# A one-layer transformer trunk on one core: norm steps handed out at other places, weight sums formed elsewhere, second attention's outputs written straight into their operand buffers

## The chip, the cores and the metric

The kernel runs on 1 core of a Trainium2 chip. The metric is the device time of one execution in microseconds (us). TensorE is PE in the profile, VectorE DVE, ScalarE ACT, GpSimd POOL, and SyncE SP; SP issues nearly all DMAs, POOL those that add to what lies at their destination.

## The reference, cut to what matters

One layer, 2048 frames, model width 1024, 16 heads of 64, feed-forward width 2816, all float32:

```python
def reference(x, g_pre_mix, g_post_mix, w_qkv, w_o, rel_bias, g_pre_ffn, g_post_ffn, w_gate, w_up, w_down):
    h = rms_norm(x, g_pre_mix[0])
    m = chunk_relpos_attention(h, w_qkv[0], w_o[0], rel_bias[0])
    x = x + rms_norm(m, g_post_mix[0])
    h = rms_norm(x, g_pre_ffn[0])
    return x + rms_norm(swiglu(h, w_gate[0], w_up[0], w_down[0]), g_post_ffn[0])
```

In the attention a chunk of 64 frames reads itself and the 8 chunks before it, with a learned bias per relative position and head: `softmax(q k / 8 + bias) v`. `swiglu` is `(silu(h w_gate) * (h w_up)) w_down`.

## The kernel before, in words

**Data.** Activations lie transposed (features on the 128 partitions) in four blocks of 512 frames, two blocks to a group `g`. A float32 product is made of three matmuls (`products`, L182): each operand is split into a rounded part `hi` and the rest `lo` (ScalarE writes `hi`, VectorE `lo`: `split`, L273, and for weights `split_part`, L129).

**Stages, in the order of TensorE.** First group: its queries, keys and values, with its attention beside them (`attend_first`, L1573, 56 to 500 us). Then output projection `o_half(0, 0)`; queries and keys of the second group (`qk_stage`, L927, about 522 to 755 us) and its values (`v_stage`, L986, to about 831 us). Second group's attention (`attend_second`, L1610, about 851 to 1256 us) with `o_half(0, 1)` beside it; `o_half(1, 0)` and `o_half(1, 1)` (to 1325 us). Then, for each group, gate and up (`gate_up`, L1059: 1325 to 1777 and 1980 to 2413 us) and down (`down`, L1152).

**Seven products for eight.** The big products (second group's queries, keys, values; gate and up; down) treat 2x2 blocks of weights A and of activations B by Strassen's scheme in Winograd's form: seven block products, named by their B side, B11, B21, T1, T2, B22, T3, T4. Four of them need sums of weight blocks: S1 = A21 + A22, S3 = A11 + A21, S2 = A11 + S1, S4 = A12 + S2. `weight_sums` (L852) makes these in DRAM: SP copies one block to the place of the sum, and POOL issues a DMA that adds the other block (`accum_op`) and has to wait for the copy. The generator gives 4 steps to each unit of weights, and whoever calls `next(sums)` issues one step, that is some copies and some additions. The units come in the order: 4 of queries and keys, 2 of values, 11 of gate and up, 11 of down. 40 steps are issued in the first attention, 8 in `qk_stage`, 14 in `v_stage`, two in three slots of the second attention (43), and the rest after it. An addition on POOL's queue is placed behind the last instruction of POOL so far, in the attentions a normalisation of probabilities (L489).

**Steps beside TensorE.** TensorE's order is written out by hand; the other engines' orders come from a scheduler which sees the program as it is written. Work that isn't matmul is handed out through the queue `later` (L190): `tick(w)` credits 1 for each product of 512 columns, and a step is written down when the credit reaches its cost. `drain()` (L202) writes down all that is left at once. `Late` (L1247) is the norm behind a projection: 8 steps `sums` (load a row of blocks, square, add up), `rstd` (two TensorE instructions at `pssq` and `prs` with a power on POOL between them, and `wait` units between the two), and 8 steps `write` (load output and residual, two vector operations, store, and with `keep` a square and an addition for the next norm). Small tiles come from rings: `io` has 3 buffers, `scratch` and `narrow` 9 in the feed-forward phase, the combined tiles of a stage lie in one `big` tile with a single buffer.

**The second attention.** 64 slots `t`, four query blocks `ib` for each of 8 pairs of heads and two blocks of frames. In a slot TensorE makes the scores (`st`, one buffer of three banks), VectorE adds the bias and takes the maximum (L481), ScalarE takes the exponential and its sum (L485), VectorE the reciprocal (L488), POOL multiplies (L489). Two slots later TensorE transposes the rows (`deep_transposed`, L540) and three slots later multiplies them with the values into the one bank `po` (`deep_output`, L563). `put` (L581) takes a finished `po`: it copies it to DRAM, to be loaded and split by `gather` (L592) when the projection is near; only the last pair goes straight into the operand buffers `ats`. `fill(t)` (L1546) interleaves `t` us of dense work. After each slot come 4 units of credit.

The kernel's code, as far as the change touches it:

## Time and profile before

| | |
|---|---|
| median of 3 runs | 2641.21 us (2634.43 to 2641.94) |
| profiled execution, its own time | 2643.79 us |
| its span | 2641.8 us |
| granted clock of TensorE, mean | 0.958 |
| busy share of the span: PE, DVE, ACT, POOL | 92%, 58%, 41%, 12% |
| moved by DMA | 564.51 MB, mean 214 GB/s |

How to read the rows that follow in the prediction. A row of a table by stretch gives the stretch in us, its length, and for each engine its busy time and number of instructions; then TensorE's granted clock (1.00 is full), the mean busy share of the core's 16 DMA engines, and GB/s. A row of waits reads: who waited at which line, for whom, us in total, times, longest. A row of a group gives line, engine, operation, out<-in, shapes, count, then busy us, the mean ns of one, and the engine's idle time before them with what ended it. A row of a timeline gives start, duration, what, and in brackets the idle time before. A matmul of 512 columns is listed with some 0.39 us, but the next one starts about 0.23 us after it, so matmuls are priced by stretches here.

### The profile page before, as it was taken

The numbers are of one execution on the slowest core, as the hardware profiler recorded it, in microseconds if no ns is written. First come the engines' busy times: TensorE is split into PE (matmuls) and PEld (weight loads), VectorE is DVE, ScalarE is ACT, GpSimd is POOL, SyncE is SP. The second block draws the span as 40 slices with busy tenths as digits, with TensorE's granted clock in tenths as the row PEclk, the third lists the DMA queues.
The fourth block names the chain that finished last, engine by engine and source line by source line (L and its number), as shares of the span: only waits on it lengthen the run. The fifth ranks groups of instructions, "written<-read, shape, count | busy, mean of one in ns | idle before, by whom it ended". The sixth has DMA issues, their size and how long they took to land.

```text
span 2641.8 us, 36015 instructions
## 1 busy us (share of the span) xinstructions
PE 2422.0 (92%) x12794; PEld 2011.7 (76%) x12794; DVE 1526.5 (58%) x2624; ACT 1091.7 (41%) x1913; POOL 321.0 (12%) x411
## 2 busy tenths in 40 slices
PE   9999998926998889479979999999999999999997
PEld 8887886715887778467768878888888888888886
DVE  6655546554544446465755675557765665555567
ACT  5444444332342446345343333336543333333444
POOL 0222222100000344233100000000000000000001
PEclk9999999967999989779989999999999999999999
DMA  7779889776899999895955675537757764456654
GB/s 219 198 209 252 209 232 254 210 232 187 264 302 263 255 229 232 231 253 130 285 183 186 223 247 179 161 119 247 251 196 234 244 207 156 151 159 219 199 186 153
DMA packets 247266, 564.51 MB, mean 214 GB/s; under 512 B 27920, under 2 KB 38176, under 8 KB 246832
## 3 DMA queue, kind: packets, MB, share of 16 engines
q1 hardware_dynamic: 230960, 515.03, 61.2%
q0 software_dynamic: 16128, 47.19, 11.0%
q8 instruction: 101, 1.65, 0.3%
q14 instruction: 77, 0.63, 0.1%
HBM read 432.30 MB, written 199.02 MB: 239 GB/s over the span
## 4 chain that ended last, share of the span: by engine, by line
PE 71%; DMA 14%; DVE 6%; issue 4%; ACT 2%; SPq 1%; POOL 1%; DVEq 0%; POOLq 0%; ACTq 0%
PE pd L185 6%; PE pd L186 6%; PE pd L184 6%; PE pb L184 5%; PE pb L185 5%; PE pb L186 5%; PE pa L184 3%; PE pa L186 3%; PE pa L185 3%; PE pc L184 3%; PE pc L186 3%; PE pc L185 3%; PE mm L184 3%; PE mm L185 3%; PE mm L186 3%
## 5 line engine op out<-in xcount | busy, mean ns | idle before, releaser
L485 ACT ACTIVATE sc<-sc,nmax 128x640 f32<-128x640 f32 (+4 forms) x256 | 193.0, 755 | 155.5 <-DVE nmax L481 146.3
L481 DVE CUSTOM_DVE_ANT_0 sc<-st,bias 128x640 f32<-128x640 f32 (+4 forms) x256 | 180.4, 738 | 129.4 <-PE st L473 115.1
L489 POOL TENSOR_SCALAR sc<-sc,rows 128x640 f32<-128x640 f32 (+4 forms) x256 | 200.2, 844 | 388.7 <-DVE rows L488 337.2
L184 PE MATMUL pb<-hb,whi_gate_up_at_T 128*128 128x512 f32 x528 | 207.1, 392 | 7.3 <-DVE terms L1104 7.3
L185 PE MATMUL pb<-hb,whi_gate_up_at_T 128*128 128x512 f32 x528 | 206.2, 390 | 0.0
L186 PE MATMUL pb<-hb,wlo_gate_up_at_T 128*128 128x512 f32 x528 | 206.0, 390 | 0.0
L184 PE MATMUL mm<-hb,whi 128*128 128x512 f32 x448 | 186.7, 417 | 0.0
L472 PE MATMUL st<-k,q 128*128 128x384 f32 (+1 forms) x448 | 140.3, 332 | 41.1 <-DVE nmax L481 29.2
L186 PE MATMUL mm<-hb,wlo 128*128 128x512 f32 x448 | 176.4, 394 | 1.6 <-DVE wlo L131 1.6
L185 PE MATMUL mm<-hb,whi 128*128 128x512 f32 x448 | 176.3, 394 | 0.0
L184 PE MATMUL pa<-hb,whi_gate_up_at_B 128*128 128x512 f32 x352 | 139.6, 397 | 12.4 <-ACT terms L1085 11.6
L258 POOL TENSOR_TENSOR rs<-ms,neg_half 128x4 f32<-128x4 f32 (+1 forms) x9 | 11.8, 1312 | 1128.4 <-DVE ms L256 1128.4
L186 PE MATMUL pa<-hb,wlo_gate_up_at_B 128*128 128x512 f32 x352 | 138.9, 395 | 3.9 <-DVE wlo_gate_up_at_B L131 3.9
L185 PE MATMUL pd<-a,whi_d_T 128*128 128x512 f32 (+1 forms) x368 | 139.9, 380 | 0.4 <-DVE a L275 0.4
L184 PE MATMUL pd<-a,whi_d_T 128*128 128x512 f32 (+1 forms) x368 | 140.0, 380 | 0.0
L186 PE MATMUL pd<-a,wlo_d_T 128*128 128x512 f32 (+1 forms) x368 | 139.7, 380 | 0.0
L185 PE MATMUL pa<-hb,whi_gate_up_at_B 128*128 128x512 f32 x352 | 138.7, 394 | 0.0
L473 PE MATMUL st<-k,q 128*128 128x384 f32 (+1 forms) x448 | 134.4, 319 | 0.0
L131 DVE TENSOR_TENSOR wlo_gate_up_at_T<-raw,whi_gate_up_at_T 128x1024 fp32r<-128x1024 f32 x88 | 107.5, 1221 | 41.2 <-ACT whi_gate_up_at_T L130 40.9
L130 ACT ACTIVATE whi_gate_up_at_T<-raw 128x1024 fp32r<-128x1024 f32 x88 | 93.1, 1058 | 91.3 <-PE pa L185 35.2
L1106 ACT ACTIVATE terms<-terms 128x512 f32<-128x512 f32 x66 | 41.7, 631 | 203.1 <-DVE terms L1104 203.1
L184 PEld LDWEIGHTS pb<-hb,whi_gate_up_at_T 128*128 128x128 f32 x528 | 99.5, 189 | 29.9 <-DVE terms L1104 9.4
(282 smaller groups left out, 6131.7 us busy)
## 6 DMA issues: line engine op xcount, KB each, us to landing
raw<-gu_S SPq DMA_DIRECT2D x88, 512.0 KB, 3.9
raw<-in_w_gu SPq DMA_DIRECT2D x66, 512.0 KB, 4.0
y<-y SPq DMA_DIRECT2D x96, 256.0 KB, 3.7
gu_S<-in_w_gu SPq DMA_DIRECT2D x44, 512.0 KB, 8.1
raw_d<-d_S SPq DMA_DIRECT2D x88, 256.0 KB, 3.4
raw_a<-aT SPq DMA_DIRECT2D x88, 256.0 KB, 3.5
aT<-T SPq DMA_DIRECT2D x66, 256.0 KB, 4.1
raw_a<-aB SPq DMA_DIRECT2D x66, 256.0 KB, 3.7
```

Source lines behind the costliest of these rows:

```text
L130: act.activation(hi, raw, AF.Copy)
L131: dve.tensor_tensor(lo, raw, hi.bitcast(F32), op=ALU.subtract)
L184: pe.matmul(pt, a_hi, b_hi, start=first, stop=False, skip_group_check=go_on)
L185: pe.matmul(pt, a_hi, b_lo, start=False, stop=False, skip_group_check=go_on)
L186: pe.matmul(pt, a_lo, b_hi, start=False, stop=last, skip_group_check=go_on)
L258: pool.tensor_tensor(r[0][:, :nb], m[:, :nb], neg_half.to_broadcast([P, nb]), op=ALU.pow)
L472: pe.matmul(st[:, a:b], q[:, 2 * h, cols], kk[:, h, key], start=True, stop=False)
L473: pe.matmul(st[:, a:b], q[:, 2 * h + 1, cols], kk[:, h, key], start=False, stop=True)
L481: dve.tensor_tensor_reduce(out=sc[:, :n], in0=st[:, c0 : c0 + n], in1=rev, scale=-1.0, scalar=3.0e38, op0=ALU.add, op1=ALU.min, accum_out= ...
L485: act.activation(sc[:, :n], sc[:, :n], AF.Exp, bias=nmax, scale=-1.0, accum_out=rows[:, 0:1])
L489: last_pool[0] = pool.tensor_scalar(sc[:, :n], sc[:, :n], rows[:, 1:2], 1.0, op0=ALU.mult, op1=ALU.mult)
L1106: act.activation(terms[0], terms[0], AF.Silu)
```

## The change

Five things, by the places where they stand.

1. **Norm of the first block's output.** In `dense`, the steps of `late` were put behind B22 in `later`, and `drain()` in the first unit of `qk_stage` wrote them down in one go. Now `qk_stage` gets `late` and puts its steps into `later` behind that `drain()`. The norm of the second block (`late1`) costs 4.0 and 8.0 per step, not 2.0 and 3.0; the norms in gate and up wait 24.0, not 6.0, between their two TensorE instructions.
2. **Sums of queries and keys.** No longer in `weight_sums` and DRAM: `qk_stream` loads the four blocks of a unit and VectorE adds them in place, four additions of 128x1024 a unit. `combined` takes two of its inputs from `narrow` instead of `io`.
3. **The other sums' places.** 40 steps in the first attention as before (now of values and gate and up), four products of a unit in `qk_stage` call for one instead of two (16 steps), `v_stage` once instead of twice for each product (7), the second attention not at all, the first group's `gate_up` at B11, T1, T2, T3 (what is left of 104 steps, down's units but for the start of the first three).
4. **Second attention's outputs.** The buffers `ats` of block (1, 0) exist from the start of the second attention, those of (1, 1) from the end of `o_half(0, 1)`. `put` splits each output straight into them from `po`, and what was spilled before that, for (1, 1), is gathered as before. The dense work runs at 1.2 us a slot instead of 0.8, 12 us of it ahead instead of 8.
5. **Reciprocals.** In the second attention one reciprocal for both heads of a slot, behind both exponentials; both normalisations stand behind it.

```diff
-sum_qk = {n: dram.tile([P, NPAIR // 2, 1024], F32, name=f"qk_{n}") for n in ("S1", "S2", "S3", "S4")}
...
 def scores(self, ib):
-                    sc[:, :n], sc[:, :n], AF.Exp, bias=nmax, scale=-1.0, accum_out=rows[:, 0:1]
+                    sc[:, :n], sc[:, :n], AF.Exp, bias=nmax, scale=-1.0, accum_out=rows[:, h : h + 1]
                 )
-                dve.reciprocal(rows[:, 1:2], rows[:, 0:1])
+                if g == 0:
+                    dve.reciprocal(rows[:, 2 + h : 3 + h], rows[:, h : h + 1])
+                elif h == 1:
+                    dve.reciprocal(rows[:, 2:4], rows[:, 0:2])
+            for h in range(2):
+                sc = self.sc[ib, h]
                 last_pool[0] = pool.tensor_scalar(
-                    sc[:, :n], sc[:, :n], rows[:, 1:2], 1.0, op0=ALU.mult, op1=ALU.mult
+                    sc[:, :n], sc[:, :n], rows[:, 2 + h : 3 + h], 1.0, op0=ALU.mult, op1=ALU.mult
                 )
...
 def put(self, po):
-            if p < NPAIR - 1 or (g, s) == (0, 1):
+            if (g, s) not in ats:
+                spilled[g, s].append(p)
                 ot = xp.tile([P, HALF], F32, tag="io", name="ot", bufs=3)
...
 def combined(self, w):
-                c[k] = [io("b11"), io("b12"), self.wait[:, k, :], self.wait[:, 4 + k, :]]
+                c[k] = [narrow("b11"), narrow("b12"), self.wait[:, k, :], self.wait[:, 4 + k, :]]
...
-    units = [qk_at(c) for c in range(NPAIR // 2)] + [v_at(u) for u in range(2)]
+    units = [v_at(u) for u in range(2)]
...
+    def qk_stream(c):
+        def add(out, a, b_):
+            dve.tensor_tensor(raw[out], raw[a], raw[b_], op=ALU.add)
...
+        makes = (
+            (("A11",), maker("B11", "A11")),
+            (("A12",), maker("B21", "A12")),
+            (("A21", "A22"), maker("T1", "A21", ("A11", "A11", "A21"), ("A21", "A21", "A22"))),
+            ((), maker("T2", "A21", ("A21", "A11", "A22"), ("A12", "A12", "A21"))),
+            ((), maker("B22", "A12")),
+            ((), maker("T3", "A11")),
+            ((), maker("T4", "A22")),
+        )
...
 def qk_stage(b, late):
-            if name in ("B22", "T4"):
+            if name in ("B11", "T1", "B22", "T4"):
                 next(sums, None)
...
             if c == 0:
                 drain()
+                later.extend(late.sums(8.0) + late.rstd(40.0) + late.write(10.0))
...
 def gate_up(g, b):
+            if g == 0 and name in ("B11", "T1", "T2", "T3"):
+                next(sums, None)
...
 def dense():
-        later.extend(own.plain(1.5, "B22") + [(0.0, lambda: later.extend(
-            pause(8.0) + late.sums(8.0) + late.rstd(40.0) + late.write(10.0)))])
-        yield from qk_stage(own)
+        later.extend(own.plain(1.5, "B22"))
+        yield from qk_stage(own, late)
...
-        later.extend(late1.sums(2.0) + late1.rstd(12.0) + late1.write(3.0))
+        later.extend(late1.sums(4.0) + late1.rstd(12.0) + late1.write(8.0))
...
-                    later.extend(late.sums(6.0) + late.rstd(6.0) + late.write(10.0))
+                    later.extend(late.sums(6.0) + late.rstd(24.0) + late.write(10.0))
...
 def finish_heads(g):
+            if g == 1:
+                ready_ = s == 0 or ("o", 0, 1) in said
...
 def attend_second():
+        finish_heads(g)
-        fill(8.0)
+        fill(12.0)
-            rate = 3.0 if t < 2 else (0.8 if t < slots - 8 else 2.4)
+            rate = 3.0 if t < 2 else (1.2 if t < slots - 8 else 2.4)
-                if t % 3 != 2:
-                    next(sums, None)
```

What the change moves on the engines, at three places.

VectorE in the query and key stage, from the fourth product on. `total` and `next` are the norm's sums, `y` and `res` its output and residual; `terms` are the products' combined results, `raw` loaded weights. Before:

```order
L962 TENSOR_TENSOR terms<-terms 128x512
L240 TENSOR_TENSOR total<-total,y 128x512 x5
L256 TENSOR_SCALAR ms<-pssq 128x4
L1271 SCALAR_TENSOR_TENSOR y<-y,gt,total 128x512 x2
L1274 TENSOR_TENSOR y<-res,y 128x512 x2
L240 TENSOR_TENSOR next<-next,sq 128x512
...
L256 TENSOR_SCALAR ms<-pssq 128x4
L961 TENSOR_TENSOR terms<-terms,pb 128x512 x2
```

Now:

```order
L923 TENSOR_TENSOR raw_5618<-raw_5618,raw_5706 128x1024
L994 SCALAR_TENSOR_TENSOR lo<-terms,hi 128x512
L923 TENSOR_TENSOR raw_5706<-raw_5706,raw_5708 128x1024
L1008 TENSOR_TENSOR terms<-pc,terms 128x512
L130 TENSOR_TENSOR wlo_qk_B_5711<-raw_5656,whi_qk_B_5710 128x1024
...
L1008 TENSOR_TENSOR terms<-pb,terms 128x512
L239 TENSOR_TENSOR total<-total,y 128x512 x2
```

Before, the whole norm stood in one piece between the sixth row of `terms` and the first that reads `pb`. Now its sums stand in ones to threes among the results of the products, and the additions of weights (L923) with them.

POOL in the second attention. `gu_S` are sums of gate and up, `sc` the rows of probabilities, `hr_ffn` and `rs` the norms' powers. Before:

```order
L489 TENSOR_SCALAR sc<-sc,rows 128x640 x2
L862 DMA gu_S_188<-in_w_gu 128x1024
...
L862 DMA gu_S_190<-in_w_gu 128x1024
L489 TENSOR_SCALAR sc<-sc,rows 128x640 x4
L862 DMA gu_S_191<-gu_S_189 128x1024
```

Now:

```order
L493 TENSOR_SCALAR sc<-sc,rows 128x640 x60
L257 TENSOR_TENSOR rs<-ms,neg_half 128x4
L493 TENSOR_SCALAR sc<-sc,rows 128x640 x38
L257 TENSOR_TENSOR hr_ffn_1_194<-ms,neg_half 128x4
L493 TENSOR_SCALAR sc<-sc,rows 128x640 x30
L867 DMA d_S_190<-in_w_d 128x512
```

The additions stood between the normalisations of nearly every slot. Now the first one, of down's sums, stands behind the last normalisation.

VectorE in the second attention, where the second norm's sums are made. `st` are scores, `pT` the transposed rows, `ot` an output on its way to DRAM, `hb` an operand buffer. Before:

```order
L481 ISA sc,nmax<-st,bias_7431 128x640
L553 COPY pT<-tt 128x4x128
L488 RECIPROCAL rows<-rows 128x1 x2
L240 TENSOR_TENSOR total<-total,y 128x512 x3
L585 COPY ot<-po 128x512
L240 TENSOR_TENSOR total<-total,y 128x512 x3
L256 TENSOR_SCALAR ms<-pssq 128x4
```

Now:

```order
L480 ISA sc,nmax<-st,bias_7651 128x640
L480 ISA nmax 128x1
L556 COPY pT<-tt 128x4x128
L490 RECIPROCAL rows<-rows 128x2
L239 TENSOR_TENSOR total<-total,y 128x512
L480 ISA sc,nmax<-st,bias_7646 128x640
```

Six of the seven additions stood in one slot, around the copy of an output. Now they stand one to a slot or two, in slots 21 to 29, and the writes behind them up to slot 49 (before: sums in 35 to 39, writes in 43 to 49).

More of the change, by code (lines that the diff above doesn't have):

```diff
@@ L590, in put @@
             said.add(("pv", g, s, p))
+    spilled = {(g, s): [] for g in range(NG) for s in range(2)}
     def gather(g, s):
         at = Cols(s)
-        for p in range(NPAIR if (g, s) == (0, 1) else NPAIR - 1):
+        for p in spilled[g, s]:
             a = xp.tile([P, HALF], F32, tag="io", name="al", bufs=3)
@@ L634, in o_half @@
                     if dt == 0:
+                        while ("pv", g, s, NPAIR - 2) not in said:
+                            yield None
                         for n in range(2):
@@ L903, in factor_stream, with loader, load, maker @@
         return load, make, 4, 3
+    def qk_stream(c):
+        raw = {}
+        def loader(*names):
+            def load():
+                for a in names:
+                    raw[a] = phase["fp"].tile([P, 1024], F32, tag="w4", name="raw4", bufs=4)
+                    sp.dma_start(raw[a], w_qk[c, BLOCK_AT[a]])
+            return load
+        def add(out, a, b_):
+            dve.tensor_tensor(raw[out], raw[a], raw[b_], op=ALU.add)
+        def maker(n, a, *adds):
+            def make(_):
+                for out, x_, y_ in adds:
+                    add(out, x_, y_)
+                w = w_tile(f"qk{c}_{n}")
+                split_part(*w, raw[a])
+                return w
+            return make
+        makes = (
[7 more added lines that the diff above has]
+        )
+        return [(loader(*names), make, 4, 3) for names, make in makes]
     def down_stream(g, n, c):
@@ L1452, in dense @@
             yield from gate_up(g, blocks[g])
+            for _ in sums:
+                pass
             drain()
@@ L1534, in trunk @@
     own = AttentionBlocks([x[2], x[3]], "qkv")
-    stream.extend(factor_stream(qk_at, c, n) for c in range(NPAIR // 2) for n in BLOCKS)
+    for c in range(NPAIR // 2):
+        stream.extend(qk_stream(c))
     stream.extend(factor_stream(v_at, u, n) for n in V_ORDER for u in range(2))
@@ L1567, in finish_heads @@
         for s in range(2):
[L1568 removed]
+            if (g, s) in ats:
                 continue
[L1570 removed]
+            if g == 1:
+                ready_ = s == 0 or ("o", 0, 1) in said
+            else:
+                ready_ = s == 0 and ("pv", g, s, NPAIR - 2) in said and ("qk", g, s, NPAIR - 1) in said
+            if ready_:
                 gather(g, s)
@@ L1637, in attend_second @@
                 job.scores(ib)
-                if t % 3 != 2:
-                    next(sums, None)
             fill(0.3 * rate)
@@ L1652, in trunk @@
     attend_second()
-    for _ in sums:
-        pass
     for c in work:
```

11 lines of the change are left out of this document (3 added, 8 removed).

## The prediction, made before the changed kernel ran

> **What bounds the kernel now.** I read the table of engine busy time by stretch first, then TensorE's waits in the stretches where it is not full, then the groups of instructions there. The profiled execution took 2643.8 us (span 2641.8). Seven rows of the table:
>
> ```profile
> core 0: us, PE busy (x) PEld busy (x) DVE busy (x) ACT busy (x) POOL busy (x), PEclk, DMA share, GB/s
> 616.00:755.00 139.00, 139.00 (x602) 114.85 (x603) 73.52 (x91) 48.83 (x66) 6.89 (x8) 0.98 0.80 241
> 850.80:1056.30 205.50, 184.98 (x1553) 157.62 (x1553) 105.75 (x283) 107.66 (x242) 79.31 (x98) 0.95 0.94 241
> 1056.30:1159.40 103.10, 54.91 (x441) 47.70 (x439) 53.52 (x114) 40.26 (x85) 29.47 (x35) 0.74 0.89 241
> 1159.40:1234.10 74.70, 66.25 (x546) 55.47 (x547) 45.25 (x113) 44.50 (x98) 29.96 (x37) 0.93 0.70 181
> 1163.00:1177.70 14.70, 14.70 (x155) 13.20 (x154) 10.20 (x32) 10.02 (x25) 6.55 (x8) 1.00 0.92 235
> 1348.00:1777.00 429.00, 422.73 (x1870) 349.49 (x1871) 257.45 (x341) 150.57 (x200) 5.36 (x4) 0.99 0.57 182
> 1777.00:1980.00 203.00, 203.00 (x897) 168.06 (x896) 142.94 (x225) 108.03 (x190) 0.00 (x0) 1.00 0.71 235
> ```
>
> TensorE bounds it wherever it is full: the rest of the query and key stage (616 to 755), gate and up (1348 to 1777), down (1777 to 1980). There one dense matmul costs 203.00/897 = 0.2263 us. Time is lost in two places. The first is around the query and key stage; the waits of TensorE between 500 and 620 us:
>
> ```profile
> PE pssq L254 <- DVE next L240: 37.2, 1, 37.2
> PE pa L184 <- ACT terms L958: 18.8, 1, 18.8
> PE pssq L254 <- DVE total L240: 13.3, 1, 13.3
> PE prs L270 <- POOL rs L258: 1.4, 1, 1.4
> ```
>
> Three of these (37.2 + 13.3 + 1.4 = 51.9 us) are the norm of the first attention output: `drain()` hands out all its steps at once in front of the product T2, and TensorE stands until their DMAs and vector work are done.
>
> The second place is the second attention (850.8 to 1234.1). Its floor is the stretch without stalls, 1163.0 to 1177.7. The score reductions count the slots (four rows of them per slot; same four stretches), and line 184 the dense work beside them (one row in three of it):
>
> ```profile
> 850.80:1056.30 205.50, 61.71 (x156) 0.95 0.94 241
> 1056.30:1159.40 103.10, 17.63 (x44) 0.74 0.89 241
> 1163.00:1177.70 14.70, 6.31 (x16) 1.00 0.92 235
> 1159.40:1234.10 74.70, 20.70 (x52) 0.93 0.70 181
> ```
>
> ```profile
> 850.80:1056.30 205.50, 23.17 (x50) 9.59 (x50) 0.95 0.94 241
> ...
> 1159.40:1234.10 74.70, 7.93 (x17) 3.28 (x17) 0.93 0.70 181
> ```
>
> So a slot costs 14.70/4 = 3.675 us of TensorE. The surplus over floor and dense work is 205.5 - 39 x 3.675 - 150 x 0.2263 = 28.3 us, then 103.1 - 11 x 3.675 = 62.7 us, then 74.7 - 13 x 3.675 - 51 x 0.2263 = 15.4 us. What ends the waits in the first, second and third of these stretches:
>
> ```profile
> PE tt L548 <- POOL sc L489: 19.5, 7, 4.6
> PE st L472 <- DMA bias<-ext_d: 10.2, 1, 10.2
> ```
>
> ```profile
> PE st L472 <- DVE nmax L481: 24.3, 4, 11.3
> PE po L574 <- DVE ot L585: 11.9, 1, 11.9
> PE pssq L254 <- DVE total L240: 7.8, 1, 7.8
> ```
>
> ```profile
> PE py L184 <- ACT hb L274: 3.9, 2, 2.8
> ```
>
> The first is GpSimd, late with the normalised rows. Its timeline shows why: the accumulating DMA stands in its queue until the copy that it adds to has landed, and four normalisations then run in one burst behind it.
>
> ```profile
> 1066.12 0.85 POOL L862 DMA_DIRECT2D d_S<-in_w_d  x1 [5.80 <-issue]
> 1066.72 3.38 POOL L489 TENSOR_SCALAR sc<-sc,rows 128x640 f32<-128x640 f32 x4
> ```
>
> The second stretch is the second norm (`late1`): its steps crowd into 11 slots and block VectorE.
>
> **The change, part by part.**
>
> *First norm handed out after the drain.* 51.9 us of waits go, and the matmuls behind them no longer run slow: 602 x (139.00/602 - 0.2263) = 2.8 us. (The Trainium skill, "TensorE: Matmul & The Clock Gate", Part 1, has the clock at half after a stop of some 3.4 us and back about 4 us into the next work: by its figures, as an estimate, one stop costs 2 us, and the sum would be 0.8 lower.) Its steps now lie beside qk products. The nearest row with such steps beside products is gate and up:
>
> ```profile
> PE pb L184 <- DVE terms L1104: 6.3, 2, 5.3
> ```
>
> ```profile
> L131 DVE TENSOR_TENSOR wlo_gate_up_at_T<-raw,whi_gate_up_at_T 128x1024 fp32r<-128x1024 f32 x88 | 107.5, 1221 | 41.2 <-ACT whi_gate_up_at_T L130 40.9
> ```
>
> 48 norm steps (32 sums, 16 writes) cost 6.3 us there, so the 16 of this norm (8 and 8) cost 2 to 3; VectorE is fuller here, so I take 6 (0 to 20). Gain 54.7 - 6 = 48.7.
>
> *Sums of queries and keys on chip.* 16 additions of 128x1024, at the 1.221 us of the nearest operation of that size, are 19.5 us of VectorE. Three units' share, 14.7, and the norm's 23.9 (as the second norm's, below) come on top of 73.52 of 139.00: 112, covered by TensorE's 139. If that cover were gone, the 14.7 would show. The first unit's four additions (4.9) stand where VectorE is what TensorE waits for (the 18.8): against them, `narrow` gives the combined inputs nine buffers for three, so loads run ahead. Net +4 (-5 to +9).
>
> *Weight sums leave the second attention.* No accumulating DMA stands among the normalisations any more. 28.3 falls to 4 (0 to 10): gain 24.3. The bias wait at its start (10.2) gets 12 instead of 8 us of dense work ahead: +6 (0 to 10). The dense work is only moved: the slots that lose it cost 3.675 each, as 1163 to 1177.7 did.
>
> *The second norm at 4 and 8 per step instead of 2 and 3.* By the order its steps now lie in slots 21 to 49, not 35 to 49. The work, and the waits of VectorE for it:
>
> ```profile
> L240 DVE TENSOR_TENSOR total<-total,y 128x512 f32<-128x512 f32 x7 | 6.8, 978 | 14.6 <-ACT y L239 14.4
> L1271 DVE SCALAR_TENSOR_TENSOR y<-y,gt,total 128x512 f32<-128x512 f32 x8 | 6.5, 813 | 10.6 <-DMA y<-yo 10.6
> L1274 DVE TENSOR_TENSOR y<-res,y 128x512 f32<-128x512 f32 x8 | 5.5, 692 | 5.2 <-DMA res<-in_x 5.1
> L240 DVE TENSOR_TENSOR next<-next,sq 128x512 f32<-128x512 f32 x7 | 5.1, 731 | 1.4 <-ACT sq L239 1.4
> ```
>
> Work 23.9 plus waits 31.8 is 55.7 us. VectorE is busy 10.20/4 = 2.55 of a slot's 3.675, so 29 slots have 32.6 us to spare: 23 are left if the waits stay as they are, none if they vanish. I take 22 (5 to 45), since TensorE's own wait for the sums (7.8) may stay in part: gain 40.7.
>
> *Outputs straight to buffers; the gathers go.* 15.4 falls to 5 (2 to 15): gain 10.4. What 14 outputs pay for it: the bank `po` is now read by two engines in turn.
>
> ```profile
> L275 DVE TENSOR_TENSOR hb<-po,hb 128x512 fp32r<-128x512 f32 x2 | 1.4, 691 | 1.0 <-ACT hb L274 1.0
> ```
>
> ```profile
> L274 ACT ACTIVATE hb<-po 128x512 fp32r<-128x512 f32 x2 | 1.2, 585 | 1.1 <-PE po L574 1.1
> ```
>
> 0.585 us more each, 8.2 if all showed. The next output is behind scores and eight transposes, so most is hidden: 3 (0 to 8). The merged reciprocal holds the first head's row until the second's exponential, and behind it on VectorE stands the next slot's score reduction, which TensorE's next scores wait for; but those start 3.675 us later, and the transposes two slots later, which covers it: 0 (if not, GpSimd's waits come back, up to the 28.3).
>
> *Sums of down beside gate and up.* Some 40 steps, each a copy and an accumulation of 0.262 MB. The queues give the price:
>
> ```profile
> q1 hardware_dynamic: 230960, 515.03, 61.2%
> q0 software_dynamic: 16128, 47.19, 11.0%
> ```
>
> 0.262 x (0.612 x 2641.8/515.03 + 0.110 x 2641.8/47.19) = 2.44 us of all 16 DMA engines a step, 98 in all. On 0.57 x 429 = 245 that makes 0.80 of the stage, the share at which 616 to 755 ran with TensorE full. Norm loads will land later: -5 (-20 to 0). GpSimd's waits for copies hold only the norms' powers there, which get 24 units' time. The stretch before it (1256 to 1348) loses the last 15 steps of the sums, and TensorE waits there for vector work on loaded blocks:
>
> ```profile
> PE pa L184 <- ACT terms L1085: 10.3, 1, 10.3
> PE pa L186 <- DVE wlo_gate_up_at_B L131: 3.9, 1, 3.9
> ```
>
> Half of these 14.2: +7 (0 to 12).
>
> **Sum**: 48.7 + 4 + 24.3 + 6 + 40.7 + 10.4 - 3 - 5 + 7 = 133.1, so 2643.8 - 133.1 = 2510.7. The profiled execution is 2.6 above the median of the three runs (2641.2): forecast 2508 us.
>
> **Rivals.**
> 1. *VectorE and GpSimd stand in each other's way (0.14).* The three `total` additions that ran beside the four normalisations above took 4.28 us, where 3 x 0.692 would be 2.1:
>
> ```profile
> 1067.95 4.28 DVE L240 TENSOR_TENSOR total<-total,y 128x512 f32<-128x512 f32 x3 [5.24 <-ACT y L239]
> ```
>
> Spread over 29 slots, every norm step meets a running normalisation. At 0.7 us for each of 30 operations, 21 more than the 22 stay, and direct outputs show their whole 8: 2508 + 21 + 5 = 2534. Against: the rows of `next` (731) and `res` (692) show hardly any delay. The Trainium skill, "SBUF — State Buffer", says of the port pair that these two engines share that it is an exclusive lock, taken for a whole instruction, also by a VectorE operation with two SBUF inputs against a GpSimd one that reads SBUF; by that rule the delay is structural and spreading the steps cannot remove it. The 978 of `total` agrees, the 692 of `res` does not.
> 2. *The DMAs of down's sums make gate and up late (0.08).* At twice the price, 4.9 us a step, the stage needs 245 + 196 = 441 of 429 and loses some 30: 2538.
> 3. *The same, to the other side (0.03).* Past 429 us each further microsecond of DMA is TensorE's. Slower than before needs 184 + 133 = 317 us for 40 steps, 7.9 a step: from there on it is slower, at 10 us a step by 83, 2725. For it: 256 KB copies of short rows beside weight loads; against it: 2.44 by the queues.
> 4. *GpSimd's lateness is not the DMAs' (0.05).* Then 28.3 stays: 2532.
>
> **How the numbers follow.** The forecast has 0.70. All bounds at their good ends would give 2456, at their bad ends 2603, and neither is likely together. The range goes to four fifths of the way to the good ends, 2468, and above it holds rivals 1, 2 and 4 with some 20 us of the terms' own spread: 2556. A difference of 0.3% is about what a measurement of this kernel tells from no change. All but rival 3 end far below it: faster 0.96, same 0.01, slower 0.03.
>
> **What would show it.** Right: no wait of tens of microseconds at `pssq` in the query and key stage; no accumulation among the second attention's normalisations, and that attention 850.8 to 1234.1 shorter by 70 or more; gate and up within 10 us of 429 at a DMA share near 0.8. Wrong: score waits behind `total`, `res` or `next` as long as now (rival 1); gate and up well over 440 (2, 3); waits for `sc` of GpSimd that remain (4).

## The result, and the profile after

The changed kernel took 2559.41 us (median of four runs, 2551.8 to 2562.25), the kernel before on the same chip 2640.81 us: a ratio of 0.9692, 95% interval 0.9666 to 0.9718. Faster, as forecast, but by 81 us instead of 133, and 3 us above the upper end of the range.

Four stretches of the changed kernel from the table by stretch (queries and keys; values and what stands before the attention's first scores; second attention; gate and up of the first group). The columns are those of the rows in the prediction.

```profile
core 0: us, PE busy (x) PEld busy (x) DVE busy (x) ACT busy (x) POOL busy (x), PEclk, DMA share, GB/s
526.00:728.40 202.40, 166.20 (x694) 135.21 (x693) 136.63 (x180) 73.82 (x107) 18.30 (x21) 0.90 0.91 268
728.40:824.40 96.00, 89.94 (x397) 74.17 (x396) 39.47 (x47) 30.80 (x40) 2.06 (x9) 0.99 0.62 187
824.40:1137.00 312.60, 287.67 (x2524) 251.15 (x2525) 187.92 (x433) 189.35 (x422) 108.57 (x128) 0.94 0.66 173
1224.10:1695.10 471.00, 436.66 (x1898) 358.06 (x1897) 265.28 (x352) 159.20 (x215) 32.88 (x38) 0.96 0.72 211
```

The same four of the kernel before:

```profile
522.40:754.80 232.40, 161.70 (x693) 133.15 (x692) 126.39 (x169) 77.09 (x110) 11.66 (x14) 0.84 0.79 233
754.80:850.80 96.00, 85.84 (x379) 70.77 (x378) 38.07 (x46) 28.62 (x38) 6.96 (x15) 0.96 0.96 288
850.80:1235.20 384.40, 307.24 (x2543) 261.90 (x2544) 205.61 (x509) 193.14 (x424) 138.74 (x170) 0.89 0.88 229
1325.10:1777.60 452.50, 432.01 (x1896) 356.31 (x1897) 271.18 (x359) 163.93 (x222) 6.18 (x5) 0.97 0.58 183
```

| stretch | before, us | after, us | gained | forecast |
|---|---|---|---|---|
| ahead of queries and keys | 522.4 | 526.0 | -3.6 | 0 |
| queries and keys | 232.4 | 202.4 | 30.0 | 48.7 + 4 = 52.7 |
| values, wait for the bias | 96.0 | 96.0 | 0 | 6 |
| second attention | 384.4 | 312.6 | 71.8 | 24.3 + 40.7 + 10.4 - 3 = 72.4 |
| rest of the projections | 89.9 | 87.1 | 2.8 | part of 7 |
| gate and up, first group | 452.5 | 471.0 | -18.5 | -5, and the rest of the 7 |
| all behind it | 864.2 | 863.7 | 0.5 | 0 |

Of the missing 50 us, 23 are in queries and keys and 18 in gate and up together with the stretch ahead of it; the bias wait (6) and the code ahead of queries and keys (4) make most of the rest. What TensorE waits for in queries and keys now:

```profile
PE pa L183 <- ACT terms L1000: 13.6, 2, 12.5
PE pssq L253 <- DVE next L239: 13.0, 1, 13.0
PE pb L183 <- DVE terms L1008: 9.6, 3, 6.6
```

The wait of 37.2 us is gone, but 13.0 of it came back at the same place, and VectorE stands at the norm's residual:

```profile
DVE y L1318 <- DMA res<-in_x: 20.4, 5, 5.6
```

Gate and up shows the same two kinds of wait, TensorE's first, then VectorE's; the third fence is VectorE's in the kernel before:

```profile
PE pb L183 <- DVE terms L1148: 21.9, 5, 8.0
PE pa L183 <- ACT terms L1129: 8.6, 2, 8.3
```

```profile
DVE y L1318 <- DMA res<-in_x: 23.6, 10, 6.1
```

```profile
DVE y L1274 <- DMA res<-in_x: 4.7, 7, 1.4
```

TensorE's wait for the products' `terms` went from 6.3 to 21.9 us, and VectorE's for the residual from 4.7 to 23.6. The products' results stand behind these residuals in VectorE's order and are late with them. How a residual comes to be late is seen in the timeline of the queries' and keys' stretch, first SP's queue, then VectorE:

```profile
677.31 0.60 SPq L70 DMA_DIRECT2D x<-y  x1
677.96 0.57 SPq L70 DMA_DIRECT2D res<-in_x  x1
678.58 0.62 SPq L70 DMA_DIRECT2D raw<-in_w_v  x1
684.76 0.33 SPq L70 DMA_DIRECT2D y<-yo  x1
```

```profile
679.17 1.23 DVE L130 TENSOR_TENSOR wlo_qk_B<-raw,whi_qk_B 128x1024 fp32r<-128x1024 f32 x1 [0.70 <-ACT whi_qk_B L129]
685.34 0.69 DVE L1318 TENSOR_TENSOR y<-res,y 128x512 f32<-128x512 f32 x1 [4.94 <-DMA res<-in_x]
```

The residual's load stands right behind the store of the step before it (SP issues both in order, and the ring `io` has three buffers), is issued at 677.96 and is used at 685.34, 7.4 us later. SP itself stands until such a store has landed, since the buffer is free only then. Its wait in gate and up, in the changed kernel:

```profile
SPq L70 <- DMA x<-y: 48.3, 14, 4.8
```

In the kernel before it was 30.1 us, also in 14 waits. (The Trainium skill, "DMA: Bandwidth & Descriptors", Anatomy of one DMA, has any semaphore wait stand on the issuing engine's sequencer before the transfer is dispatched; these waits agree.)

The second attention shows what the forecast asked for: no wait for GpSimd's `sc` is left.

```profile
PE st L471 <- DVE nmax L480: 13.0, 3, 7.9
PE st L471 <- DMA bias<-ext_d: 6.1, 1, 6.1
PE pssq L253 <- DVE total L239: 4.5, 1, 4.5
```

### The profile page after: what moved, and what is told of

Its sections match the earlier page's. It is cut to its first block, busy times and chain, and to the rows that moved or that the text cites. A ratio compares the mean times of both kernels' runs of the same rounds, so it can differ in the third digit from the quotient of the medians.

```text
span 2558.8 us, 35820 instructions
## 1 busy us (share of the span) xinstructions
PE 2415.6 (94%) x12794; PEld 2008.1 (78%) x12794; DVE 1522.6 (60%) x2564; ACT 1087.1 (42%) x1913; POOL 312.6 (12%) x395
## 4 chain that ended last, share of the span: by engine, by line
PE 43%; DMA 6%; DVE 3%; issue 1%; ACT 1%; SPq 0%; DVEq 0%; POOL 0%; ACTq 0%
PE pd L184 5%; PE pd L183 5%; PE pd L185 5%; PE pb L183 4%; PE pb L184 4%; PE pb L185 4%; PE pa L183 3%; PE pa L184 2%; PE pa L185 2%; PE pc L183 2%; PE pc L184 2%; PE pc L185 2%; DMA y<-y 2%; DMA x<-y 2%; DMA res<-in_x 1%
```

## The experiments

Theory (transfers): where steps of down's and the other weight sums stand beside products and norm steps, the norm's loads land late, and through VectorE's order the products' results do. Rivals: the places that the moved norm steps take on VectorE; the ring of three buffers by itself; VectorE's additions on chip. The code ahead of queries and keys is the same in all the runs with the change but took 515 to 528 us, so parts are compared by stretches of the profiled executions, and the whole by ratios to the kernel before on the same chip. A stretch is read from one execution and has a spread of its own, seen where several runs have the same code in it: queries and keys with sixteen steps 202 to 210 us (eleven runs), the second attention as changed 308 to 313 (seven), gate and up with its sums 467 to 472 (five, mean 470.4) and without them 444.5 to 452 (five, mean 448.5). Differences within such a spread are not told apart here. All edits are against the changed kernel unless another run is named.

### Beside the queries' and keys' products

**Eight steps of sums there instead of sixteen.**

```diff
-            if name in ("B11", "T1", "B22", "T4"):
+            if name in ("B22", "T4"):
...
+            next(sums, None)          # v_stage, a second step a product
```

> The changed kernel with 8 steps of sums in the query and key stage, not 16, and 14 in the value stage, not 7, as before the change. Transfers theory: the query and key stage (526 to 728, 202 us) falls by 8 to 15 us, its VectorE wait for res from 20.4 to below 12, and the value stage stays at 76 us; total 2544 to 2552. If VectorE's own work (the additions of weights) makes that stage long, not transfers: the stage stays within 4 us of 202.

```profile
520.70:702.60 181.90, 161.65 (x693) 132.82 (x692) 137.33 (x182) 74.07 (x108) 13.13 (x14) 0.93 0.85 262
```

Ratio 0.9615 (0.9589 to 0.9641). The stretch loses 20.5 us (20 to 28 by the spread of the sixteen), more than expected, and the values' row, which takes seven of the steps, is at 95.0 (96.0 in the changed kernel); VectorE's wait for the residual falls from 20.4 to 9.4, the wait at `pssq` from 13.0 to 4.1. VectorE is as busy as before the edit (137.33 against 136.63), so it was not its own work.

**None there**, fourteen more calls beside the values' products than in the changed kernel (the trace has 18 copies there instead of 6, and 12 in the run with eight), the rest in gate and up.

```diff
-            if name in ("B11", "T1", "B22", "T4"):
+            if name in ():
...
+            next(sums, None)          # v_stage, two more calls
```

> The changed kernel with none of the steps of down's sums in the stretch of the queries' and keys' products: five or six more go beside the values' products, the rest stay in gate and up. With sixteen the stretch took 202.2 us, with eight 182.0. If what is lost there is the transfers' doing (2.5 us for each step moved), it comes to 162 to 172 us, down to the products' own 152 at the least, and VectorE's waits for the norm's loads go from 9.4 to under 4 us. If what is left at eight is VectorE's own work (the additions of the weight sums on chip, 19.5 us, and the norm's steps), it stays at 178 to 182. The values' stage gets more transfers: 76.4 us if its share of .55 leaves room for them, 80 to 88 if not. Gate and up as in the changed kernel, 471 and up to 8 more, as it keeps more of the sums. The whole: 2530 to 2542 by the first, 2537 to 2552 by the second.

```profile
524.90:696.90 172.00, 157.25 (x694) 129.46 (x693) 137.19 (x181) 74.44 (x107) 5.58 (x5) 0.96 0.72 229
696.90:800.70 103.80, 89.91 (x398) 74.18 (x396) 39.30 (x47) 30.04 (x40) 9.17 (x11) 0.95 1.00 297
800.70:1131.10 330.40, 287.10 (x2525) 250.21 (x2526) 188.48 (x433) 189.19 (x422) 112.24 (x139) 0.93 0.66 167
```

Ratio 0.9674 (0.9638 to 0.971). The stretch falls by another 9.9 us: 1.2 us a step for the first eight, 2.6 (2.5 to 3.5) for the second eight. But the values' row, at a DMA share of 1.00, loses 8, and the attention behind it 18. TensorE's two waits at the attention's start, and behind the first of them VectorE's:

```profile
PE st L471 <- DVE nmax L480: 17.7, 1, 17.7
PE st L471 <- DMA q<-qk: 13.9, 1, 13.9
```

```profile
DVE sc L480 <- POOL bias L333: 32.8, 1, 32.8
```

The 13.9 us for the queries end the values' row, where the wait for the bias was 6.1: that is its loss. The 17.7 are the attention's loss: on GpSimd additions, issued up to 821.71 us, stand ahead of the `memset` pairs at L332 and L333 that prepare the bias, and the first scores' maximum (822.93) waits for the first pair; in the changed kernel all four pairs were done by 811.4. So the 18 us come from the place of the additions in GpSimd's queue.

**The norm's steps alone**, on the kernel before.

```diff
-    def qk_stage(b):
+    def qk_stage(b, late):
...
+                later.extend(late.sums(8.0) + late.rstd(40.0) + late.write(10.0))
...
-        later.extend(own.plain(1.5, "B22") + [(0.0, lambda: later.extend(
-            pause(8.0) + late.sums(8.0) + late.rstd(40.0) + late.write(10.0)))])
+        later.extend(own.plain(1.5, "B22"))
...
```

> The kernel before with only the first norm's steps handed out behind the drain, one part of the change alone; queries and keys still load their sums whole, and eight steps of down's sums stand beside them as before. The forecast put 48.7 us on this part, with 6 us of new waits. If the forecast's sum for the part stands by itself, the stage falls from 232 to about 184 us and the whole to 2588 (2583 to 2595). If the stage's loads of sums made beforehand (a DMA share of .79 before) make the norm's own loads late, as down's sums did in the changed kernel, half is lost again: 195 to 215 us, the whole 2600 to 2620.

```profile
516.30:712.10 195.80, 162.40 (x694) 131.65 (x693) 124.46 (x171) 76.72 (x113) 12.17 (x13) 0.92 0.89 273
```

Ratio 0.9846 (0.9793 to 0.9899). 36.6 us for the 48.7 forecast, in the expectation's second case. Beside the run with eight steps (181.9), the weight sums on chip and the nine buffers are then worth 13.9 where the forecast had 4: with eight steps in both, the two terms make 50.5 of the 52.7.

### Beside gate and up

**The sums back in the second attention.**

```diff
-            if g == 0 and name in ("B11", "T1", "T2", "T3"):
-                next(sums, None)
...
+                if t % 3 != 2:
+                    next(sums, None)
```

> The changed kernel with one part undone: the sums that are left after the value stage are issued in the second attention again (two slots in three, the rest behind it), none in gate and up. Transfers theory (the sums' DMAs make the loads of the norm beside gate and up land late, VectorE stands at them and TensorE behind it): gate and up of the first group falls from 457 us (1238 to 1695) to about 430, VectorE's wait for res there from 23.6 to about 5; the second attention, 311.5 us now, grows by the 28 us that stood under GpSimd's waits before, so the total is about the same as the changed kernel's 2559, 2545 to 2575. Places theory (the norm's steps were moved to worse places by the longer pause of 24): gate and up stays at 450 or more and the total goes to about 2585. GpSimd rival of the prediction: the attention doesn't grow, and the total falls to about 2535.

```profile
824.50:1154.50 330.00, 286.01 (x2525) 247.98 (x2526) 191.88 (x433) 189.34 (x422) 135.78 (x168) 0.93 0.86 223
1241.60:1686.10 444.50, 431.14 (x1898) 355.13 (x1897) 265.61 (x352) 159.90 (x215) 4.44 (x4) 0.98 0.57 182
```

Ratio 0.968 (0.9649 to 0.971): gate and up gains 26.5, the attention loses 17.4. The places of the norm steps are the same, so this is the sums' doing: 26.5 us between these two runs, some 22 between the means with and without.

**The norms' statistics at 6 units again.**

```diff
-                    later.extend(late.sums(6.0) + late.rstd(24.0) + late.write(10.0))
+                    later.extend(late.sums(6.0) + late.rstd(6.0) + late.write(10.0))
```

> The changed kernel with the norms in gate and up waiting 6 units again, not 24, between their two TensorE instructions. Transfers theory: gate and up stays within 5 us of 457, total within 6 us of 2559. Places theory: gate and up falls by 15 us or more, to about 440, total about 2543.

Ratio 0.9659 (0.9637 to 0.968). Gate and up took 459.0, 12 less (8 by the lowest of the five): between the two expectations.

**The norms' loads from the ring of nine.**

```diff
-                y, res = io("y"), io("res")
+                y, res = (narrow("y"), narrow("res")) if "fp" in phase else (io("y"), io("res"))
```

> The changed kernel with the two loads of a norm's write step taken from the ring of nine (narrow) instead of the ring of three (io) in the feed-forward phase. Ring theory (with three buffers a step's load can't be issued before an earlier result's store has landed, and SP stands at it with the weight loads behind): VectorE's wait for res falls from 23.6 and 20.4 us in gate and up and in the query and key stage to below 8 each, the two stages lose 25 to 40 us together, total 2520 to 2535. Transfers theory without the ring (the DMA engines themselves are late): the waits stay, total within 8 us of 2559.

```profile
1226.70:1671.50 444.80, 430.43 (x1898) 355.52 (x1897) 265.14 (x353) 159.74 (x217) 32.80 (x38) 0.98 0.75 223
```

Ratio 0.9614 (0.9594 to 0.9634). Gate and up gains 26.2 us, at least as much as without the sums, with all transfers in place. SP's wait for landed stores, 48.3 us above, is down to 3.0. In the queries' and keys' stretch the same edit gains nothing: 209.1 us, at the upper end of the spread. VectorE's wait moves on to the loads of `y` there, and SP waits 21.9 us for the norm's results (8.7 before this edit); why it does so there was not found:

```profile
DVE y L1315 <- DMA y<-yo: 26.9, 5, 6.7
```

**The ring of nine without the sums** (the first edit of this group and, from gate and up on, the third).

> The run with gate and up's sums back in the second attention (gate and up 444.5 us with the ring of three), and on top the norms' loads from the ring of nine from gate and up on. It completes a table of four: sums there and ring of three 471, sums and nine 443 to 445, no sums and three 444.5. If the ring of three only costs where transfers are slow, this run gains nothing: gate and up 440 to 445, the whole 2546 to 2551. If the two costs are separate and only happened to be of one size, gate and up falls by another 15 to 20, to 425 to 430, and the whole to 2531 to 2536.

```profile
1245.60:1679.00 433.40, 426.93 (x1898) 352.92 (x1897) 265.73 (x352) 160.05 (x215) 4.44 (x4) 1.00 0.58 184
```

Ratio 0.962 (0.959 to 0.965). In between the expectations: without sums the ring of three costs 11.1 us (15.1 by the mean of 448.5), with the ring of nine the sums cost 9.9 to 11.4, and together they cost 37.6, so some 11 to 17 arise only where both meet.

**Copies without additions.**

```diff
-                steps[4 * u + n].append((add, dst[to], a))
+                if u < 2 + NC:
+                    steps[4 * u + n].append((add, dst[to], a))
```

> The changed kernel with the additions into the sums of down's weights left out; the copies stay (down then multiplies by copied blocks instead of sums, so its numbers are others, its work the same). By the queues a copy is 0.82 us of the 2.44 of a step, an addition 1.61. If what makes the norm's loads late in gate and up is the volume of transfers, the loss of 26 us falls to about a third of it: gate and up 450 to 456, the whole 2540 to 2545. If it is the copies' places in SP's queue ahead of the loads, little changes: 465 to 471, the whole 2553 to 2560. If the additions alone do it, gate and up is at 444, the whole at 2533.

```profile
1216.50:1666.50 450.00, 432.58 (x1898) 355.82 (x1897) 265.31 (x352) 159.76 (x215) 4.43 (x4) 0.98 0.62 199
```

Ratio 0.959 (0.9564 to 0.9616). The copies' places in SP's queue are not what costs: they are still there, and the 465 to 471 us that this would give did not come. 450.0 is at the edge of what the volume of transfers would give (450 to 456), but also within the 444.5 to 452 of the runs without any sums, so whether the volume or the additions as such make the loads late stays open. The medians from issue to landing of the residual's loads in gate and up (name, queue, count, KB, us) follow; the changed kernel first, then the copies alone, then the kernel before:

```profile
res<-in_x SPq DMA_DIRECT2D x16, 256.0 KB, 5.7
```

```profile
res<-in_x SPq DMA_DIRECT2D x16, 256.0 KB, 4.8
```

```profile
res<-in_x SPq DMA_DIRECT2D x16, 256.0 KB, 4.5
```

### Both mended

**Eight steps, and the ring of nine from gate and up on.** The edit is that of the run with eight steps, and the ring's with the condition `"gu" in said`, which is set ahead of `gate_up`.

> The changed kernel with two things altered: eight of the sixteen steps of down's sums leave the stretch of the queries' and keys' products again (the last sums stage of the run of eight slots before it and the values' products take them as in the kernel before), and the norms' write steps take their two loads from a ring of nine narrow buffers instead of the ring of three, but only from the first gate and up on, where the run with the narrow ring in every stage gained; in the queries' and keys' stage it lost 7 us, so there they stay in the ring of three. If the two losses are separate (the loads of the norm late behind down's sums in one stage, and the ring of three stores in the other), the gains add: queries and keys' stretch about 182 us (20 under the changed kernel), gate and up of the first group about 445 (26 under), the whole about 2559 - 46 = 2513 us (2508 to 2520). If both runs gained from one and the same thing, which only shows in one place at a time (the whole was 2535 in either), the sum stays at 2530 to 2537.

```profile
517.50:700.80 183.30, 161.85 (x693) 132.95 (x692) 139.33 (x184) 75.86 (x110) 13.42 (x14) 0.93 0.85 258
1193.80:1637.10 443.30, 429.00 (x1897) 353.95 (x1896) 264.90 (x352) 159.67 (x215) 33.68 (x39) 0.99 0.75 224
```

2510.84 us, ratio 0.9511 (0.9469 to 0.9554): the gains add.

**With the statistics at 6 on top.**

> The run with both mendings and, on top, the statistics' steps in gate and up at 6 again as in the kernel before, instead of 24: with the ring of three the 6 was 12 us shorter. If that difference came from where the norm's loads meet down's sums in the ring of three, nothing of it is left with the ring of nine: gate and up within 3 us of the run without it, the whole within 4 us of it. If it comes from VectorE's own places (a step nearer to the products' terms holds them up), 8 to 12 us are gained again, and the whole is about 2503.

Ratio 0.9548 (0.9512 to 0.9584), gate and up 453.2: 9.9 us more. The pitch of 6 was 12 us better with the ring of three and is 10 worse with the ring of nine; neither expectation had that, and why the sign changes stays open.

**The last eight steps into gate and up too**, shown against the run with both mended.

```diff
-            if name in ("B22", "T4"):
-                next(sums, None)
...
-            if g == 0 and name in ("B11", "T1", "T2", "T3"):
+            if g == 0 and name in ("B11", "T1", "T2", "B22", "T3"):
```

> The run with both mendings, and the last eight of down's sums taken out of the queries' and keys' stage as well, into gate and up, which calls for five steps a unit instead of four; the values' stage keeps its 14. By the run with none there (172 us) the queries' and keys' stage gains 10 to 11 us, by the price in gate and up with the ring of nine ((443.3 - 433.4)/40, 0.25 us a step) gate and up loses 2 to 4: the whole 2502 to 2505 beside 2510.8. If the values' stage gets steps that the queries' and keys' stage no longer takes first and is late with its own sums, it gains nothing.

```profile
518.80:691.30 172.50, 158.13 (x694) 130.03 (x693) 138.81 (x183) 76.55 (x111) 6.39 (x6) 0.96 0.72 230
1182.40:1628.00 445.60, 428.14 (x1897) 353.55 (x1896) 267.79 (x356) 162.28 (x220) 40.32 (x47) 0.98 0.79 235
```

2506.37 us, ratio 0.9511 (0.9479 to 0.9543). By stretches 10.8 us gained in queries and keys and 2.3 lost in gate and up, as expected; the whole cannot be told from that of the run with both mended. These two are the fastest versions, 1.9% under the changed kernel by the ratios.

### In the second attention

The sum of the terms came out there, so each term was undone. The edits: the norm's pitch (`late1.sums(2.0)`, `late1.write(3.0)`); the outputs spilled (the old `finish_heads`); the sums in the attention (above); and all of them together.

> The changed kernel with the second norm's steps at 2 and 3 units again, as before, instead of 4 and 8. The forecast put 40.7 us on the wider pitch (62.7 us of surplus to 22). If that term stands by itself, the second attention goes from 312 to about 352 us and the whole to 2600 (2590 to 2605). The rival: the crowded steps were dear before mainly because additions of weights, copies to DRAM and gathers stood among them, which are gone now; then only a part comes back, 5 to 20 us, the whole 2565 to 2580.

> The changed kernel with the second attention's outputs spilled to DRAM and gathered again as before (the old conditions of finish_heads); everything else as changed. The forecast put 10.4 - 3 = 7.4 us on the straight outputs: the second attention about 320 us, the whole 2566 (2559 to 2573). If the copies to DRAM were part of what blocked VectorE in the crowd of the second norm, more comes back here: 10 to 20 us.

> The changed kernel with the outputs spilled and gathered and the second norm at 2 and 3 as well. By itself the pitch was worth 5 us of the second attention (312.6 to 317.6), the spilling 26.8 (339.4). If each cost stands by itself, both together give 344 us. If the crowded norm is dear only where copies to DRAM and gathers stand in the same queues (the 62.7 us of the kernel before), 355 to 375 us, and the whole 2598 to 2615.

> The changed kernel with the outputs spilled and the weight sums in the second attention again, the norm at the wider pitch. One by one they cost 26.8 and 17.3 us of the second attention: added, 357 us. If either hides behind the other, 340 to 347; if they meet in the same queues, 362 to 372. Gate and up without sums as measured without them, 444.

> All three undone: outputs spilled, sums in the second attention, norm at 2 and 3; the second attention is then that of the kernel before except for 12 instead of 8 us of dense work ahead, 1.2 instead of 0.8 a slot and the merged reciprocals. It should be near the 384 us of before (375 to 385) if those three make the whole gain of 72. One by one they make 49 (26.8 + 17.3 + 5.0): 362 if they only add, and then some 20 us of the gain belong to the pace of the dense work or the reciprocals, to which the forecast gave 6 and 0.

| the attention with | us | ratio of the whole |
|---|---|---|
| the change | 312.6 | 0.9692 (0.9666 to 0.9718) |
| pitch undone | 317.6 | 0.9719 (0.968 to 0.9759) |
| outputs spilled | 339.4 | 0.9794 (0.9751 to 0.9837) |
| sums there | 330.0 | 0.968 (0.9649 to 0.971) |
| spilled, pitch undone | 334.3 | 0.9816 (0.9796 to 0.9836) |
| spilled, sums there | 363.5 | 0.9818 (0.9784 to 0.9852) |
| all three undone | 359.6 | 0.9794 (0.9768 to 0.982) |
| kernel before | 384.4 | 1 |

The pitch is worth 5.0 us with straight outputs (up to 9 by the spread), and nothing beside spilled ones (-5.1; 334.3 is below both expectations) and sums (-3.9). Spilling costs 26.8, more than expected, or 33.5 beside the sums (363.5 - 330.0). All three undone make 47 of the 71.8. The other 24.8 were looked for in the rest of the change, each edit on top of all three: a reciprocal for each head, and the old pace (8 us ahead, 0.8 a slot).

> The run with outputs spilled, sums in the second attention and the norm at 2 and 3 (second attention 359.6 us, where the kernel before has 384.4), and on top a reciprocal for each head, each normalisation behind its own, as in the kernel before. Only the pace of the dense work (12 ahead, 1.2 a slot) is then left of the change in this attention. If the merged reciprocal makes the 24.8 us that are left over, the attention is at 380 to 386 and the whole at 2596 to 2602; if the pace makes them, as the forecast's 6 and 0 would rather have it, the attention stays at 357 to 364 and the whole at 2573 to 2582.

> The same run of three undone parts with the pace of the dense work as before instead (8 us ahead, 0.8 a slot) and the merged reciprocal kept. If the pace makes the 24.8 us: second attention 380 to 386 us, with the wait for the bias at its start 4 us longer and the outputs' crowd at its end back. If the reciprocal makes them: 357 to 364. If the two share them: both runs near 370.

```profile
826.10:1177.50 351.40, 297.41 (x2525) 257.50 (x2526) 204.32 (x508) 189.86 (x422) 139.15 (x168) 0.91 0.86 227
```

```profile
824.70:1194.60 369.90, 302.55 (x2542) 259.30 (x2543) 201.44 (x446) 193.96 (x424) 136.47 (x168) 0.91 0.84 216
```

Ratios 0.9773 (0.9756 to 0.9789) and 0.98 (0.9775 to 0.9824). The pace makes 10.3 us; the merged reciprocal gains nothing (351.4 without it, 8.2 less than with it). So 14.5 us of the attention's gain are not assigned to a single part, 22.7 if the reciprocal's 8.2 are counted; where they come from stays open.

## Why the prediction was wrong, point by point

- **What failed first: a step without a price.** Part 3 of the change puts sixteen steps of sums beside the queries' and keys' products where eight were. The prediction priced such steps in gate and up alone. Eight of them cost 20.5 us here (202.4 against 181.9), nearly all of the 22.7 that this stretch fell short. The stretch had shown a DMA share of 0.79 before, the sums on chip take loads away, and I counted that room as gain without counting who takes it.
- **What failed second: the cover of down's sums.** "-5 (-20 to 0)", argued by a share of 0.80 "at which 616 to 755 ran with TensorE full". The price was good: 33 copies at 0.82 and 34 additions at 1.61 make 82 us of transfers, and 0.72 x 471.0 - 0.57 x 444.5 gives 86. The share came out below 0.80, at 0.72. The row came out 18.5 longer all the same, and the sums' part was some 22 to 26.5, since that stretch of reference had no norm step in it: no load on which VectorE waits in order, behind a store in a ring of three (SP's 48.3 us for 30.1). In this case the share told whether the transfers fit, not when a single one landed (5.7 us for 4.5).
- **First norm, 48.7.** Mechanism right, size 36.6; the "2 to 3, I take 6" for its steps beside products was 12 too low, within the bound of 20; one run alone shows it, with eight steps of sums beside the norm.
- **Sums on chip, +4.** 13.9, beyond the bound of 9. The additions took the 19.5 us expected, wholly covered:

```profile
L923 DVE TENSOR_TENSOR raw<-raw,raw 128x1024 f32<-128x1024 f32 x16 | 19.5, 1217 | 5.7 <-DMA raw<-in_w_qk 5.7
```

- **Second attention, 72.4.** 71.8, but by other terms: the norm's pitch 5.0 instead of 40.7, straight outputs 26.8 instead of 7.4, weight sums 17.4 instead of 24.3, the pace 10.3. The whole surplus of the slots in which the norm stood was put down to the norm; the runs put 26.8 to 33.5 us on what else stood there, copies to DRAM and gathers, and leave 14.5 or more open. The pitch was not undone alone on the kernel before. That the sum is right is chance.
- **Bias wait, +6.** It fell from 10.2 to 6.1, and the 4 us were spent on the dense work ahead of it: 96.0 before and after. **Stretch ahead of gate and up, +7**: 2.8, and the waits at the start of gate and up from 14.2 to 8.6, so 8.4.
- **Rival 1, VectorE against GpSimd: not seen at its size.** In slots full of normalisations the norm's operations take

```profile
L1315 DVE SCALAR_TENSOR_TENSOR y<-y,gt,total 128x512 f32<-128x512 f32 x8 | 6.0, 756 | 2.2 <-DMA y<-yo 1.6 <-ACT total L270 0.6
L239 DVE TENSOR_TENSOR total<-total,y 128x512 f32<-128x512 f32 x7 | 5.6, 799 | 3.8 <-ACT y L238 3.7
L1318 DVE TENSOR_TENSOR y<-res,y 128x512 f32<-128x512 f32 x8 | 5.6, 695 | 7.3 <-DMA res<-in_x 7.2
L239 DVE TENSOR_TENSOR next<-next,sq 128x512 f32<-128x512 f32 x7 | 5.3, 754 | 0.7 <-ACT sq L238 0.6
```

  0.05 us more on average than the same operations in the queries' and keys' stretch (744, 688, 689 and 689 ns), not 0.7. The means hide single ones: of the 30 operations 11 lay beside a normalisation, six of these took 0.07 to 0.46 us longer, 1.5 us in all, and five did not. (The lock of the Trainium skill, "SBUF — State Buffer", SBUF: two separate sides, would hold an operation for what is left of a normalisation of 0.859 us; the six may show it, the five do not.)
- **Rival 2** had the size (some 30 us in gate and up, where its own 441 us in 429 give only 12) and the wrong reason: not twice the price, but lateness at the forecast price. **Rivals 3 and 4** did not come: no 7.9 us a step, no wait for `sc`. **The range**: four fifths of the way from 2508 to 2456 is 2466, not 2468.

## What to carry to other kernels

When background transfers are moved, price them at every place to which they go, and ask there which in-order engine waits for a load issued behind a store: the mean DMA share said here whether they fit, not whether that load was late. A deeper ring for just those loads took back 26 us with every transfer left in place, though it gained nothing in another stage. Ask also what stands behind the moved work in the queue of the engine that issues it. A surplus read off a stretch belongs to all that stands in it; before the whole of it is given to one step, see which part of it that step's own rows carry.

## What the runs showed that was not expected

- At the same number of steps the price of a moved step grows: 1.2 us for each of the first eight beside the queries' and keys' products (share 0.72 to 0.85), 2.6 for the next eight (0.85 to 0.91). With none of them there, the 18 us lost in the second attention were not the DMA share's: the preparation of the bias stood behind the moved additions on GpSimd.
- With the ring of nine (the run with both mended, gate and up) a residual takes nearly as long to land (5.4 us for 5.7), but VectorE waits for it less than half as long (9.3 for 23.6):

```profile
res<-in_x SPq DMA_DIRECT2D x16, 256.0 KB, 5.4
```

```profile
DVE y L1319 <- DMA res<-in_x: 9.3, 5, 3.7
```
